# First attention of a hybrid diffusion step: queries kept in SBUF, key stacks moved into the last mLSTM scan, the prompt block's eight heads in one score tile

## The chip, the cores and the metric

The kernel runs on one core of one Trainium2 chip. The metric is the device time of one execution in microseconds (us), the median over the runs. TensorE (PE) multiplies matrices, VectorE (DVE) and GpSimd (POOL) do elementwise work and reductions, ScalarE (ACT) does activations and copies, SyncE (SP) issues most DMAs. PEld is the loading of weights into TensorE.

## The reference

One layer of a diffusion transformer over 128 prompt tokens and 1024 latent tokens, with attention heads and mLSTM heads side by side. In the reference's words, shortened:

```
h = rmsnorm(x, norm1_w) * (1 + sc1) + sh1
aq, ak, av, mq, mk, mv, mo, mg = split(h @ w_in)
aq = rmsnorm(aq, q_norm_w);  ak = rmsnorm(ak, k_norm_w)      # 8 query heads, 2 key heads, 64 wide
latent tokens:  aq = rope(aq); keys = [rope(ak), cache_k]; vals = [av, cache_v]   # 1024 + 128 keys
prompt tokens:  keys, vals = ak, av                                               # 128 keys, no rope
attn_o = softmax(aq keys^T / 8) vals
hm     = rmsnorm(mlstm_forward(..) + mlstm_backward(..)) * sigmoid(mo)            # 4 heads, 128 wide
x = x + g1 * ([attn_o, hm] @ w_out)
x = x + g2 * swiglu(rmsnorm(x, norm2_w) * (1 + sc2) + sh2)
```

Everything is float32. Most products are made from two halves (a high part and the rest), so one product is three matmuls.

## The kernel before, in words

The 1152 tokens are nine blocks of 128: block 0 is the prompt, blocks 1 to 8 are latent. Three blocks make a chunk. The program is built by Python generators that are woven into one another (`weave(main, side, n, m)` takes m steps of the side for n of the main), and a scheduler then orders the instructions of each engine; `hot()` raises the priority of what is written inside it. Tiles come from pools, where a tile with the same tag waits until an earlier one is no longer read.

The stages are: modulation of the conditioning, normalised input, key/value/gate projection, four mLSTM heads (the projection of one woven with the scan of the one before), then the part that the change touches:

- `linear_tok(w_q, ...)` projects the queries, 24 matmuls of 128x512 for a block. QFIRST (blocks 0 and 1, 2, 3) is woven with the last scan, `head_mlstm(3)`. QREST (4, 5 and 6, 7 and 8) comes later, woven with `key_stacks` and the first attention. `evac_q` copies a block out of PSUM (ACT, L696, tile `qraw`), `norm_rope` normalises and rotates it (a square on ACT L636, a sum on DVE L638, scaling on POOL L640, two half products on DVE L651 for each block, a product on POOL L657, a sum on DVE L658), and SP's queue writes the result to DRAM (`q_d`).
- `key_stacks` transposes the keys on PE and splits them into two halves in `kst` (casts on ACT L957 and L958, differences on DVE by the helper `sub`, L135).
- `attention(0)` treats blocks 0, 1 and 2. For a block it reads `qr` back from `q_d` by a DMA on ACT's queue, transposes it (PE L114) and splits it into `qT` (ACT L994, DVE L135). A head makes scores `S` on PE (L1016), a maximum (DVE L1018), an exponential (ACT L1019), a scaled half `ph` (ACT L1022), the rest `pl` (DVE L1023), and two transposing DMAs, `phT` and `plT`. Once both heads of a pair are through, the values follow on PE (L1040, L1041) into `po`. There is one score tile `S` of three banks and one bank for `po`; four banks `mm` serve everything else. For the prompt block a head is 128x128, for a latent block 128x1152.
- `prefill` multiplies the mLSTM half of the output projection for all nine blocks (PE L1138 to L1140). It evacuates through three small buffers (tag `t2`): DVE multiplies by the gate (L1095) and POOL adds to `x` (L1096). A product, its DVE evacuation and its POOL addition follow one another in each engine's own order.
- `attn_out(0)` adds the attention half for blocks 0 to 2 (POOL L1190), `norm2` normalises each block for the FFN (ACT L1251, transposes, L1259 on ACT for one column block in four of a half and L1261 on DVE for the others), and `gate_up_pair` starts the FFN early. The rest of attention 0 is taken in steps of `prefill` and `attn_out`, 0.7 of them for each step of attention. Attention 1 is woven into `attn_out` (0.3 of its steps for each one) and into the FFN groups behind it.

## Time and profile before

| | |
|---|---|
| median of 3 runs | 1628.43 us (1624.75, 1628.43, 2519.12) |
| profiled execution | 1623.65 us, its span 1621.9 us |
| mean granted PE clock | 0.973 |
| PE, DVE, ACT, POOL busy | 93%, 59%, 45%, 37% |
| DMA moved | 232.71 MB, of it HBM written 11.69 MB |

The span is what the profile shows of one execution, from its first instruction to its last; the execution's own time is 1.75 us longer. In the timeline a row gives the start, the duration, the engine, line, operation, `out<-in`, and in brackets how long the engine stood idle before it and what ended the idle time. In a table by windows each engine has its busy time and number of instructions; PEclk is the granted clock of TensorE (1.00 is full).

### The profile page before, as it was taken

How to read it: one execution, taken by the hardware profiler on the slowest of the kernel's cores; microseconds unless marked ns; L12 is line 12 of the kernel's file. 1: busy time of each engine (PE TensorE's matmuls, PEld its weight loads, DVE VectorE, ACT ScalarE, POOL GpSimd, SP SyncE). 2: the span in 40 equal slices, each digit the busy share in tenths (PEclk: the TensorE clock that was granted, in tenths of full speed). 3: DMA queues.
4: the chain of work that ended last, by engine and by line, in shares of the span. 5: the costliest groups of instructions: out<-in, count | busy, mean ns of one | idle time of the engine just before them, and what ended most of it. 6: DMA issues, size and time to landing. Idle time of an engine off the chain costs nothing. (4 is left out here: it accounts for less than half of the span.)

```text
span 1621.9 us, 23339 instructions
## 1 busy us (share of the span) xinstructions
PE 1513.3 (93%) x8688; PEld 1256.2 (77%) x8688; DVE 955.2 (59%) x1887; ACT 730.7 (45%) x1251; POOL 602.4 (37%) x363
## 2 busy tenths in 40 slices
PE   5899999899679867999999999999999999999996
PEld 2755666576347656998989999898898989899995
DVE  3844355847876667577663546777664474332445
ACT  3744343444444455545643344565552453333332
POOL 0411021413343414443445354443344444544443
PEclk8899999999889979999999999999999999999998
DMA  9345363302245755777763556787684445535441
GB/s 353 121 143 134 99 143 63 97 6 44 87 163 120 194 119 113 172 184 177 183 174 115 148 153 215 189 179 177 153 185 126 130 141 177 150 124 149 143 129 67
DMA packets 386311, 232.71 MB, mean 143 GB/s; under 512 B 169910, under 2 KB 346502, under 8 KB 386198
## 3 DMA queue, kind: packets, MB, share of 16 engines
q1 hardware_dynamic: 384342, 228.04, 52.6%
q10 hardware_dynamic: 1856, 3.19, 0.6%
q8 instruction: 68, 1.11, 0.3%
q14 instruction: 45, 0.37, 0.1%
HBM read 181.16 MB, written 11.69 MB: 119 GB/s over the span
## 5 line engine op out<-in xcount | busy, mean ns | idle before, releaser
L135 POOL TENSOR_TENSOR wlo<-raw,whi 128x1024 fp32r<-128x1024 f32 x146 | 360.9, 2476 | 435.6 <-ACT whi L152 404.5
L152 ACT CAST whi<-raw 128x1024 fp32r<-128x1024 f32 x219 | 224.1, 1025 | 357.9 <-DMA raw<-in_w_gu_dram 126.8
L1288 PE MATMUL mm<-aTl,whi 128*128 128x384 f32 (+2 forms) x1088 | 363.6, 334 | 0.7 <-POOL aTl L135 0.7
L1289 PE MATMUL mm<-aTh,wlo 128*128 128x384 f32 (+2 forms) x1088 | 363.4, 334 | 0.0
L1287 PE MATMUL mm<-aTh,whi 128*128 128x384 f32 (+2 forms) x1088 | 362.2, 335 | 0.8 <-DVE tn L1315 0.8
L1288 PEld LDWEIGHTS mm<-aTl,whi 128*128 128x128 f32 x1088 | 204.9, 188 | 1.7 <-POOL aTl L135 0.9
L1287 PEld LDWEIGHTS mm<-aTh,whi 128*128 128x128 f32 x1088 | 204.5, 188 | 2.2 <-DVE tn L1315 1.4
L1289 PEld LDWEIGHTS mm<-aTh,wlo 128*128 128x128 f32 x1088 | 204.9, 188 | 0.2
L135 DVE TENSOR_TENSOR wlo<-raw,whi 128x1024 fp32r<-128x1024 f32 (+1 forms) x73 | 86.7, 1188 | 145.5 <-ACT whi L152 145.3
L1106 PE MATMUL mm<-whi,hl 128*128 128x512 f32 x372 | 147.0, 399 | 1.4 <-DVE tn L1315 1.3
L1107 PE MATMUL mm<-wlo,hl 128*128 128x512 f32 x372 | 147.6, 398 | 0.0
L1108 PE MATMUL mm<-whi,hl 128*128 128x512 f32 x372 | 144.7, 397 | 0.7 <-POOL hl L135 0.7
L1023 DVE SCALAR_TENSOR_TENSOR pl<-pr,st,ph 128x1152 f16<-128x1152 f32 (+1 forms) x72 | 111.9, 1556 | 52.7 <-ACT ph L1022 51.0
L1019 ACT ACTIVATE pr<-S,st 128x1152 f32<-128x1152 f32 (+1 forms) x72 | 81.2, 1128 | 114.8 <-DVE st L1018 108.5
L488 PE MATMUL wi<-ipair,hT 128*128 128x384 f16 (+2 forms) x392 | 127.5, 326 | 2.9 <-ACT ipair L216 2.8
L489 PE MATMUL wi<-ipair,hT 128*128 128x384 f16 (+2 forms) x392 | 127.4, 325 | 0.0
L490 PE MATMUL wi<-ipair,hT 128*128 128x384 f16 (+2 forms) x392 | 126.8, 324 | 0.0
L135 POOL TENSOR_TENSOR hl<-tn,hl 128x384 fp32r<-128x384 f32 x66 | 82.8, 1256 | 106.9 <-ACT hl L1319 106.0
L1096 DVE TENSOR_TENSOR x<-x,t 128x512 f32<-128x512 f32 x102 | 116.7, 1167 | 0.8
L1315 DVE SCALAR_TENSOR_TENSOR tn<-tn,mm 128x384 f32<-128x384 f32 (+2 forms) x68 | 36.7, 540 | 136.3 <-PE mm L1289 93.5
L1016 PE MATMUL S<-kst,qT 128*128 128x384 f32 (+1 forms) x400 | 87.2, 353 | 13.5 <-ACT pr L1019 13.4
L1018 DVE TENSOR_REDUCE st<-S 128x1 f32<-128x1152 f32 (+1 forms) x72 | 88.8, 1233 | 16.7 <-PE S L1016 16.5
(353 smaller groups left out, 2639.5 us busy)
## 6 DMA issues: line engine op xcount, KB each, us to landing
raw<-in_w_gu_dram SPq DMA_DIRECT2D x132, 512.0 KB
raw<-in_w_down_dram SPq DMA_DIRECT2D x60, 512.0 KB
a<-in_w_ada_dram SPq DMA_DIRECT2D x32, 512.0 KB
gl<-g_d SPq DMA_DIRECT2D x36, 256.0 KB
aw<-in_w_ada_dram SPq DMA_DIRECT2D x16, 512.0 KB
iraw<-in_w_in_dram SPq DMA_DIRECT2D x32, 256.0 KB
raw<-in_w_out_dram SPq DMA_DIRECT2D x15, 512.0 KB
x<-in_x_sample_dram SPq DMA_DIRECT2D x13, 512.0 KB
```

The source lines that it names most:

```text
L135: (dve if eng == "dve" else pool).tensor_tensor(out=out, in0=full, in1=hi, op=ALU.subtract)
L152: nc.scalar.copy(hi[:, :n], raw[:, :n])
L488: mm(ps[:, :n], ah, wh[:, k % 2, c0 : c0 + n], start=(k == 0), stop=False)
L489: mm(ps[:, :n], ah, wl[:, k % 2, c0 : c0 + n], start=False, stop=False)
L490: mm(ps[:, :n], al, wh[:, k % 2, c0 : c0 + n], start=False, stop=(k == KD - 1))
L1096: eng.tensor_tensor(out=x1[:, cs], in0=x1[:, cs], in1=t, op=ALU.add)
L1106: mm(ps, ah, wh[:, k % 2, :], start=(k == 0), stop=False)
L1107: mm(ps, ah, wl[:, k % 2, :], start=False, stop=False)
L1108: mm(ps, al, wh[:, k % 2, :], start=False, stop=(k == nk - 1))
L1287: mm(ps, wh[:, k, :], th[:, k, :], start=(k == 0), stop=False)
L1288: mm(ps, wh[:, k, :], tl[:, k, :], start=False, stop=False)
L1289: mm(ps, wl[:, k, :], th[:, k, :], start=False, stop=(k == KD - 1))
```

## The change

- QFIRST loses block 3, which joins block 4 in QREST.
- The queries no longer go through DRAM: `evac_q` keeps them in tiles in SBUF (`q_first` for blocks 0 to 2, `qk` for each pair of the others).
- For QREST the half products and the last sum of `norm_rope` are issued on POOL instead of DVE.
- `key_stacks` is woven into the last scan; it was woven into QREST. The pools `po` and `S` are opened as soon as the scan's own PSUM pool closes, and the four `mm` banks stay open.
- The prompt block's eight heads become one tile: 16 score matmuls, one maximum, one subtraction, one exponential, one sum, one scaling, one copy, one difference, two transposing DMAs.
- `qT` has two buffers; the transposes of blocks 0, 1 and 2 are issued straight behind the scan, those of a later block when the block ahead is at its fifth head.
- The rate of `prefill` and `attn_out` beside attention 0 goes from 0.7 to 1.0.
- `norm2` gives ACT three column blocks in four for chunk 0; it was one.

```
-QFIRST = [(0, 1), (2,), (3,)]
-QREST = [(4,), (5, 6), (7, 8)]
+QFIRST = [(0, 1), (2,)]
+QREST = [(3, 4), (5, 6), (7, 8)]
...
-    psum = {"mm": es_b.enter_context(tc.tile_pool(name="pB", bufs=4, space=PSUM, reuse_waits="tile"))}
+    psum = {"mm": ctx.enter_context(tc.tile_pool(name="pB", bufs=4, space=PSUM, reuse_waits="tile"))}
...
-    def norm_rope(qp, cc, ss, x, nb, nh, w, rb):
+    def norm_rope(qp, cc, ss, x, nb, nh, w, rb, eng=dve):
...
-                dve.tensor_tensor(
+                eng.tensor_tensor(
                     out=t4[:, :, :, 16 * f : 16 * f + 16],
...
-        dve.tensor_tensor(out=x[:, skip:], in0=x[:, skip:], in1=t2[:, skip:], op=ALU.add)
+        eng.tensor_tensor(out=x[:, skip:], in0=x[:, skip:], in1=t2[:, skip:], op=ALU.add)
...
             act(qr[:, b - grp[0]], ps.rearrange("p (h d) -> p h d", d=HD), AF.Copy, scale=vsc[:, 2:3])
+            q_of[b] = qr[:, b - grp[0]].rearrange("p h d -> p (h d)")
...
-                for i, bb in enumerate(grp):
-                    dma(q_d[bb], qr[:, i].rearrange("p h d -> p (h d)"))
...
-    weave(linear_tok(w_q, 0, 512, ev_q, QFIRST), scan, 24, 60)
-    emit(scan)
...
+    ev_q = evac_q(qp, cc, ss, qw, lambda grp: q_first[:, grp[0] : grp[-1] + 1], dve)
+    weave(linear_tok(w_q, 0, 512, ev_q, QFIRST), beside((scan, 3.0), (key_stacks(), 0.2)), 16, 16)
+    es_a.close()
+    for name, bufs in (("po", 1), ("S", 1)):
+        psum[name] = ctx.enter_context(tc.tile_pool(name="p" + name, bufs=bufs, space=PSUM, reuse_waits="tile"))
+    emit(scan)
...
+        def turned(b):
+            qT = ap.tile([P, NQ, P], F32R, name=nm("qT"), tag="qT", bufs=2)
+            ps = bank()
+            for j in range(4):
+                transpose(ps[:, j * P : (j + 1) * P], q_of[b][:, j * P : (j + 1) * P])
...
+        def prompt_heads(qT):
+            S = psum["S"].tile([P, 3, 512], F32, name=nm("S"), tag="S")
+            for h in range(NQ):
+                for t in range(2):
+                    mm(S[:, h // 4, h % 4 * P : (h % 4 + 1) * P], qT[:, h, :], kst[h // 4][:, t, NB * P : (NB + 1) * P],
+                       start=(t == 0), stop=(t == 1))
...
+            dve.tensor_reduce(out=st[:, 0], in_=Sv, axis=AX.X, op=ALU.max, negate=True)
+            dve.tensor_tensor(out=p3, in0=Sv, in1=bc(st[:, 0], 2, [P, NQ, P]), op=ALU.add)
+            act(pr, pr, AF.Exp)
+            dve.tensor_reduce(out=st[:, 1], in_=p3, axis=AX.X, op=ALU.add)
+            dve.reciprocal(st[:, 0], st[:, 1])
+            dve.tensor_scalar(out=st[:, 1], in0=st[:, 0], scalar1=2.0 ** 14, scalar2=None, op0=ALU.mult)
+            dve.tensor_tensor(out=p3, in0=p3, in1=bc(st[:, 1], 2, [P, NQ, P]), op=ALU.mult)
+            nc.scalar.copy(ph, pr)
+            sub(pl, pr, ph, "dve")
...
+            dma_t(hT8, ph)
+            dma_t(lT8, pl)
...
+                    if h == 4 and b + 1 in blocks and b + 1 not in qTs:
+                        qTs[b + 1] = turned(b + 1)
...
-    weave(linear_tok(w_q, 0, 512, ev_q, QREST, bank), chain(key_stacks(), att), 24, 11)
+    next(att)
+    next(att)
+    ev_q = evac_q(qp, cc, ss, qw, lambda grp: ap.tile([P, 2, NQ, HD], F32, name=nm("qk"), tag="qk", bufs=3), pool)
+    weave(linear_tok(w_q, 0, 512, ev_q, QREST, bank), att, 24, 9)
...
-                    if j == 0 and c == 0:
+                    if j < 3 and c == 0:
...
-        due += 0.7
+        due += 1.0
```

Three places show what the scheduler makes of it. Each kernel's rows bear its own line numbers: in the changed kernel the helpers and `linear_tok` lie one line higher (L113, L134, L487), the rotation is L639, L650, L656 and L657 (before L640, L651, L657, L658), the addition to `x` is L1142 (before L1096), and L1025 to L1035 are in `prompt_heads`.

PE at the end of the last scan, before. `mm_4763` is block 4's query product, `mm_4773` and `mm_4792` are key transposes, `mm_4662` the scan's last product, `mm_4865` the first transpose of block 0's queries, `mm_4998` the first product of block 7.

```order
L846 MATMUL mm_4662<-va_4204,sd_4638 128x129 x2
L488 LDWEIGHTS hT_287
L488 MATMUL mm_4763<-ipair_4220,hT_287 128x512
...
L114 MATMUL mm_4773<-ident,kall 128x128 x4
...
L114 MATMUL mm_4792<-ident,kall 128x128 x4
...
L490 MATMUL mm_4855<-ipair_4231,hT_288 128x512
L114 MATMUL mm_4865<-ident,qr_4862 128x128 x4
L488 LDWEIGHTS hT_288
L488 MATMUL mm_4998<-ipair_4220,hT_288 128x512
```

PE at the same place in the changed kernel. `mm_4624` is the last key transpose, `mm_4682` the scan's last product, `mm_4730`, `mm_4740` and `mm_4784` are the transposes of blocks 0, 1 and 2, `mm_4793` and `mm_4794` the products of blocks 3 and 4, `mm_4936` and `mm_4937` those of 5 and 6, `S_4749` the prompt's scores.

```order
L113 MATMUL mm_4624<-ident,kall 128x128 x2
...
L844 MATMUL mm_4682<-va_4195,sd_4616 128x129 x2
L113 MATMUL mm_4730<-ident,q_first 128x128 x4
L113 MATMUL mm_4740<-ident,q_first 128x128 x4
L113 MATMUL mm_4784<-ident,q_first 128x128 x4
...
L489 MATMUL mm_4793<-ipair_4222,hT_278 128x512
L1025 MATMUL S_4749<-kst_4226,qT_4729 128x128 x2
...
L489 MATMUL mm_4794<-ipair_4218,hT_278 128x512
...
L1025 MATMUL S_4749<-kst_4227,qT_4729 128x128 x8
...
L489 MATMUL mm_4936<-ipair_4211,hT_278 128x512
L487 MATMUL mm_4937<-ipair_4211,hT_279 128x512
```

The key transposes now lie ahead of the scan's last product. Block 3's 24 products, which lay inside the scan before, stand behind it. The query transposes stand straight behind the scan instead of behind block 6, and the 16 prompt scores stand among block 4's products.

DVE behind the scan in the changed kernel. `rt_4698` and `ry_4697` belong to the root of the last mLSTM head's norm, `vs` to the values, `qT_4729`, `qT_4739` and `qT_4783` to the transposed queries of blocks 0, 1 and 2, `st_4771` and `pr_4768` to the prompt's softmax, `nrs_4910` to the norm of blocks 3 and 4.

```order
L130 SCALAR_TENSOR_TENSOR ry_4697<-rt_4698,ry_4697 128x9
L970 CAST vs<-vall 128x10x64 x2
L134 TENSOR_TENSOR qT_4729<-mm_4730,qT_4729 64x4x128
L134 TENSOR_TENSOR qT_4739<-mm_4740,qT_4739 64x4x128
L134 TENSOR_TENSOR qT_4729<-mm_4730,qT_4729 64x4x128
L134 TENSOR_TENSOR qT_4739<-mm_4740,qT_4739 64x4x128
L1032 TENSOR_REDUCE st_4771<-S_4749 128x8
L134 TENSOR_TENSOR qT_4783<-mm_4784,qT_4783 64x4x128
L1033 TENSOR_TENSOR pr_4768<-S_4749,st_4771 128x1024
L637 TENSOR_REDUCE nrs_4910<-nr_963_4908 128x16
L134 TENSOR_TENSOR qT_4783<-mm_4784,qT_4783 64x4x128
```

Before, twelve differences of `kst` stood at this place on DVE, and the first `qT` followed behind block 4's norm, the values and the norm's sum of blocks 5 and 6. Now the second half of `qT_4783`, which frees the bank of `mm_4784`, stands behind the reduction of blocks 3 and 4.

POOL at the start of `prefill` in the changed kernel. `qk_5033` and `qk_5178` are the queries of blocks 5 and 6 and of 7 and 8, `nr` their half products, `x_1019` and `x_1020` the residual sums with `t` from the DVE evacuation.

```order
L1142 TENSOR_TENSOR x_1019_5217<-x_1019_5217,t_1050_5327 128x512
L639 TENSOR_TENSOR qk_5033<-qk_5033,ry_5041 128x1024
L650 TENSOR_TENSOR nr_993_5057<-qk_5033,ss_4205 128x16x16 x3
L134 TENSOR_TENSOR kst_4227<-oT_4831,kst_4226 128x512
L650 TENSOR_TENSOR nr_993_5057<-qk_5033,ss_4205 128x16x16
L1142 TENSOR_TENSOR x_1019_5217<-x_1019_5217,t_1057_5362 128x512
...
L656 TENSOR_TENSOR qk_5033<-qk_5033,cc_4204 128x1024
L1142 TENSOR_TENSOR x_1019_5217<-x_1019_5217,t_1072_5448 128x512
L657 TENSOR_TENSOR qk_5033<-qk_5033,nr_993_5057 128x1024
...
L639 TENSOR_TENSOR qk_5178<-qk_5178,ry_5186 128x1024
```

Before, only the products of L640 and L657 stood here between the additions; now the half products (L650) and the sums (L657) of the rotation stand between them too.

More of the change, by code (lines that the diff above doesn't have):

```diff
@@ L98, in hybrid_step @@
     drp = ctx.enter_context(tc.tile_pool(name="drp", bufs=1, space=DRAM, reuse_waits="tile"))
-    es_b = ExitStack()
-    psum = {"mm": es_b.enter_context(tc.tile_pool(name="pB", bufs=4, space=PSUM, reuse_waits="tile"))}
+    psum = {"mm": ctx.enter_context(tc.tile_pool(name="pB", bufs=4, space=PSUM, reuse_waits="tile"))}
     def bank():
         return psum["mm"].tile([P, 512], F32, name=nm("mm"), tag="mm")
-    q_d = [drp.tile([P, 512], F32, name=f"q_d{b}") for b in range(NB)]
+    q_of = {}
     hm_d = drp.tile([TOK, 512], F32, name="hm_d")
@@ L686, in k_work, with evac_q @@
         yield
[L688 removed]
+    def evac_q(qp, cc, ss, qw, new, eng):
         held = {}
@@ new lines, in values @@
+        def values(i, j, nk, kv, rhs):
+            if j == 0:
+                oT.append(new_oT())
+            with hot(hv):
+                po = psum["po"].tile([P, 512], F32, name=nm("po"), tag="po")
+                for n in range(nk):
+                    v = vs[:, NB if nk == 1 else n, kv].rearrange("p t d -> p (t d)")
+                    for t in range(2):
+                        mm(po[:, 0:256], v, rhs(t, n), start=(n == 0 and t == 0), stop=(n == nk - 1 and t == 1))
+                ol = ap2.tile([64, 256], F32, name=nm("ol"), tag="ol", bufs=1)
+                act(ol, po[64:128, 0:256], AF.Copy, scale=vsc[64:128, 1:2])
+                for g in range(2):
+                    dve.scalar_tensor_tensor(out=oT[i][64 * g : 64 * g + 64, j, :],
+                                             in0=po[0:64, g * P : (g + 1) * P], scalar=vsc[0:64, 1:2],
+                                             in1=ol[:, g * P : (g + 1) * P], op0=ALU.mult, op1=ALU.add)
+            if j == 3:
+                done.add(i)
@@ L996, in attention @@
+        blocks = list(range(c * CB, (c + 1) * CB))
+        qTs = {}
+        with hot(ha):
+            for b in blocks[0:2] if c == 0 else blocks[0:1]:
+                qTs[b] = turned(b)
+        yield
+        for i, b in enumerate(blocks):
+            with hot(ha):
+                if b == 0:
+                    prompt_heads(qTs[b])
+                    qTs[2] = turned(2)
             yield
+            if b == 0:
+                continue
+            qT = qTs[b]
             for h in range(NQ):
+                kv = h // 4
+                if h % 2 == 0:
+                    while len(late) > 1:
+                        late.pop(0)()
@@ L1013, in attention @@
                     S = psum["S"].tile([P, 3, 512], F32, name=nm("S"), tag="S")
-                    for n in range(parts):
+                    for n in range(3):
                         for t in range(2):
-                            mm(S[:, n, 0:w], qT[:, h, :], kst[kv][:, t, c0 + n * w : c0 + (n + 1) * w], start=(t == 0), stop=(t == 1))
-                    Sv = S[:, 0:parts, 0:w]
+                            mm(S[:, n, 0:CT], qT[:, h, :], kst[kv][:, t, n * CT : (n + 1) * CT], start=(t == 0), stop=(t == 1))
@@ L1027, in attention @@
+                    dma_t(phT[:, h % 2, :, :], ph.rearrange("p a b -> p (a b)"))
+                    dma_t(plT[:, h % 2, :, :], pl.rearrange("p a b -> p (a b)"))
+                    if h == 4 and b + 1 in blocks and b + 1 not in qTs:
+                        qTs[b + 1] = turned(b + 1)
                 yield
-                if late and h % 2 == 1:
-                    late.pop()()
-                    yield
                 if h % 2 == 1:
-                    def values(phT=phT, plT=plT, kv=kv, nk=nk, b=b, i=i, j=h // 2):
-                        if j == 0:
-                            oT.append(new_oT())
-                        with hot(hv):
-                            po = psum["po"].tile([P, 512], F32, name=nm("po"), tag="po")
-                            for n in range(nk):
-                                vi = 9 if b == 0 else n
-                                v = vs[:, vi, kv].rearrange("p t d -> p (t d)")
-                                mm(po[:, 0:256], v, phT[:, :, n, :], start=(n == 0), stop=False)
-                                mm(po[:, 0:256], v, plT[:, :, n, :], start=False, stop=(n == nk - 1))
-                            ol = ap2.tile([64, 256], F32, name=nm("ol"), tag="ol", bufs=1)
-                            act(ol, po[64:128, 0:256], AF.Copy, scale=vsc[64:128, 1:2])
-                            for g in range(2):
-                                dve.scalar_tensor_tensor(out=oT[i][64 * g : 64 * g + 64, j, :],
-                                                         in0=po[0:64, g * P : (g + 1) * P], scalar=vsc[0:64, 1:2],
-                                                         in1=ol[:, g * P : (g + 1) * P], op0=ALU.mult, op1=ALU.add)
-                        if j == 3:
-                            done.add(i)
-                    late.append(values)
@@ L1051, in attention @@
+                    for _ in range(2 if len(late) > 2 else 1):
+                        if late:
+                            late.pop(0)()
+                            yield
+                    late.append(lambda i=i, j=h // 2, kv=kv, two=(phT, plT): values(i, j, NB, kv, lambda t, n: two[t][:, :, n, :]))
         late.pop()()
```

83 lines of the change are left out of this document (37 added, 46 removed).

## The prediction

> **What bounds the kernel now.** I read the page first: its chain of waits accounts only for the time from 1182 us on, so it says nothing on the stage that changes. The busy times by windows do.
>
> ```profile
> span 1621.9 us, 23339 instructions
> PE 1513.3 (93%) x8688; PEld 1256.2 (77%) x8688; DVE 955.2 (59%) x1887; ACT 730.7 (45%) x1251; POOL 602.4 (37%) x363
> ```
> ```profile
> core 0: us, PE busy (x) PEld busy (x) DVE busy (x) ACT busy (x) POOL busy (x), PEclk, DMA share, GB/s
> 390.90:414.60 23.70, 20.34 (x141) 15.42 (x140) 19.85 (x58) 12.76 (x43) 7.76 (x6) 1.00 0.12 37
> 414.60:457.50 42.90, 31.36 (x141) 14.91 (x140) 34.67 (x86) 15.55 (x38) 18.84 (x12) 0.88 0.33 112
> 457.50:500.00 42.50, 30.14 (x127) 22.84 (x126) 31.52 (x72) 19.14 (x42) 15.96 (x9) 0.84 0.54 158
> 500.00:554.40 54.40, 50.75 (x262) 41.52 (x261) 36.49 (x57) 27.27 (x36) 21.45 (x14) 0.97 0.64 144
> 554.40:628.00 73.60, 51.92 (x260) 41.31 (x259) 50.87 (x97) 41.33 (x58) 23.76 (x14) 0.84 0.63 137
> 663.00:1015.00 352.00, 351.19 (x1940) 323.86 (x1940) 214.78 (x308) 165.18 (x222) 151.45 (x76) 1.00 0.63 169
> 1040.00:1600.00 560.00, 556.36 (x3030) 513.98 (x3028) 293.99 (x406) 234.52 (x309) 253.02 (x123) 1.00 0.55 149
> ```
>
> From 663 us on PE is busy for 351.19 of 352 and 556.36 of 560 us, so work that is ready earlier there finds PE taken, and a microsecond won or lost ahead of it moves the end by one. Ahead of it PE has room. I cut the stage where the program does: A, the last scan (390.9 to 414.6); B, the query projection (to 457.5, where `prefill` begins); C, `prefill` (to 554.4); D, `attn_out` (to 628). In B, C and D PE stands idle for 11.5, 16.0 and 21.7 us, and half its clock is withheld for parts of the rest (0.84 to 0.88).
>
> What it waits for is seen in PE's timeline.
>
> ```profile
> 421.35 0.38 PE L490 MATMUL mm<-ipair,hT 128*128 128x512 f16 x1
> 424.88 0.58 PE L488 MATMUL mm<-ipair,hT 128*128 128x512 f16 x1 [3.15 <-ACT qraw L696]
> 427.39 0.46 PE L488 MATMUL mm<-ipair,hT 128*128 128x512 f16 x1
> 427.68 0.38 PE L489 MATMUL mm<-ipair,hT 128*128 128x512 f16 x1
> 436.32 0.38 PE L490 MATMUL mm<-ipair,hT 128*128 128x512 f16 x1
> 444.69 1.09 PE L114 MATMUL mm<-ident,qr 128*128 128x128 f32 x4 [7.99 <-DMA qr<-q_d]
> 471.12 0.69 PE L1016 MATMUL S<-kst,qT 128*128 128x128 f32 x2 [3.13 <-ACT pr L1019]
> 577.09 1.77 PE L1016 MATMUL S<-kst,qT 128*128 128x384 f32 x6 [2.80 <-ACT pr L1019]
> ```
>
> B holds a wait of 3.15 us for a free bank and one of 7.99 us for the query's way through DRAM. C begins with the prompt's heads, each waiting for the exponential of the one ahead (3.13 us), and D goes by heads of block 2 in the same way (2.80 us).
>
> At full clock the projection's matmuls follow at 0.216 us (427.68 to 436.32, 40 steps), so a block of 24 takes 5.2 us. Behind a wait they take 0.43: six from 424.88 to 427.39, about 1.3 us lost. [...]
>
> **B, what goes.** Both waits, 11.1 us, and what they slowed behind them. The round trip is certainly gone: no instruction reads or writes `q_d`. SP's queue loses those writes, and with them a wait that held all loads behind it:
>
> ```profile
> SPq L701 <- DVE qraw L658: 22.0, 3, 14.4
> ```
>
> It also issues two transposing DMAs for the prompt, not sixteen. I count that at nothing: weights arrived in time before.
>
> **A and B, what comes.** Three things.
>
> First, the scan. The twelve differences of `kst` move into it on DVE, and block 3's norm and rotation leave it.
>
> ```profile
> L135 DVE TENSOR_TENSOR kst<-mm,kst 64x512 fp32r<-64x512 f32 x8 | 5.5, 688 | 0.2
> L135 DVE TENSOR_TENSOR kst<-mm,kst 64x256 fp32r<-64x256 f32 x4 | 1.7, 422 | 0.1
> L651 DVE TENSOR_TENSOR nr<-qraw,ss 128x256 f32<-128x256 f32 x16 | 8.7, 594 | 3.3 <-POOL qraw L640 3.3
> L658 DVE TENSOR_TENSOR qraw<-qraw,nr 128x1024 f32<-128x1024 f32 x2 | 2.7, 1368 | 0.0
> L638 DVE TENSOR_REDUCE nrs<-nr 128x16 f32<-128x1024 f32 x2 | 2.4, 1220 | 0.8 <-ACT nr L636 0.8
> L636 ACT ACTIVATE nr<-qraw 128x1024 f32<-128x1024 f32 x2 | 2.1, 1052 | 4.2 <-DVE qraw L658 4.2
> L696 ACT ACTIVATE qraw<-mm,vsc 128x512 f32<-128x512 f32 x5 | 3.3, 685 | 6.5 <-PE mm L490 4.4 <-issue 2.0
> L994 ACT CAST qT<-mm 64x512 fp32r<-64x512 f32 x8 | 4.7, 582 | 5.9 <-PE mm L114 3.1 <-DVE qT L135 1.6 <-PE S L1016 1.1
> L135 DVE TENSOR_TENSOR qT<-mm,qT 64x512 fp32r<-64x512 f32 x8 | 5.5, 687 | 0.4 <-ACT qT L994 0.2
> ```
>
> 5.5 + 1.7 = 7.2 us come (these rows, and all by line that follow, are from 390 to 663 us where nothing else is said); the casts of `kst` go to ACT, busy for 12.76 of 23.7 us, and the transposes to PE, which has 3.4 us idle. Two half products (1.2), half of a 1.368 us sum, half of a 1.220 us reduction and the small root steps go, about 3.4 us. DVE was busy for 19.85 of A's 23.7 us, so the scan goes at its pace: the 3.8 us net are taken whole, and the scan ends at about 418 instead of 414.2. (Bounds: 0 if PE's slack hides them, 7.2.)
>
> Second, the first `qT`. Its tile's first cast on ACT waits for POOL: in the order it stands behind POOL's last product of the scan's output (L869). That row before, and two that stand close to it:
>
> ```profile
> 422.11 0.99 POOL L869 TENSOR_TENSOR hm<-hm,so 128x384 f32<-128x384 f32 x1
> 433.72 2.11 POOL L872 TENSOR_TENSOR hm<-hm,ry 128x1152 f32<-128x1152 f32 x1 [10.61 <-DVE ry L127]
> 423.38 0.17 DVE L129 TENSOR_TENSOR rt<-ry 128x9 f32<-128x9 f32 x1
> 433.74 2.11 DVE L129 TENSOR_TENSOR rt<-ry 128x8 f32<-128x8 f32 x1
> ```
>
> It ended 8.9 us behind the scan's end (423.1 against 414.2), so at about 426.9 now. A cast (0.58), block 3's evacuation, which stands between the casts on ACT (0.69), the second cast (0.58) and a difference (0.69) follow: block 4's products, which need that bank, start near 429.7. PE has the three transposes (about 2 us) and block 3's 5.2 us until 425.1 and two scores, so it waits about 4 us. (Bounds: 0, if another wait paces the tile, and the 7.99 us of before.)
>
> Third, the bank of `mm_4784`. Block 4's 24 products (5.2 us), 14 scores (2.4, estimated from 0.69 for two at half clock) and the slowed start (1.3) end at 438.6. `mm_4937` then waits for an evacuation (0.69), a square (1.05), a reduction (1.22) and a difference (0.69), with 0.2 to 0.3 between engines 4.6 us, of which three products of block 5 cover 0.65: about 4 us again, until 442.6. (Bounds: 0, if the difference goes ahead of the reduction, and 8, the largest wait of B.) Then 45 products remain of 5 and 6 and 48 of 7 and 8 (20.1 us), three latent heads' scores and some values (5.7, by the 1.77 us for six scores), 1.3 of slowed start. `prefill` starts at 442.6 + 27.1 = 469.7: **12 us later** than before. For that, all prompt heads and three latent ones are behind it.
>
> **C.** Busy time here is 30.14 + 50.75 = 80.9 us; with the slowed part taken out about 76. Six prompt heads go and one latent head comes (ten instead of nine), which makes 77.7.
>
> ```profile
> L1018 DVE TENSOR_REDUCE st<-S 128x1 f32<-128x1152 f32 x9 | 12.2, 1354 | 2.1 <-PE S L1016 2.0
> L1018 DVE TENSOR_REDUCE st<-S 128x1 f32<-128x128 f32 x8 | 2.3, 286 | 2.5 <-PE S L1016 2.5
> L1023 DVE SCALAR_TENSOR_TENSOR pl<-pr,st,ph 128x128 f16<-128x128 f32 x8 | 5.9, 745 | 3.9 <-ACT ph L1022 2.3 <-DMA plT<-pl 1.6
> ```
>
> The eight small chains on DVE, 2.3 + 5.9 and their small steps, 10.6 us, become two reductions (1.22 each), a subtraction (1.38), a scaling and a difference (1.37 each): 6.9 us, once. The first of these rows is of stage C. What made the first half of C slow, one small chain behind another, goes with them. The second half, 500 to 554.4, has only latent heads and 3.65 us idle in 54.4, 7%. At that share C has 5.6 us idle and some 2 of slowed clock: **85.5 us instead of 96.9**. (Bounds: 78 with none, 96.9 unchanged.)
>
> What rides on that is POOL, with twelve half products and three sums that it has not done before. The nearest rows are POOL's own products and additions.
>
> ```profile
> L657 POOL TENSOR_TENSOR qraw<-qraw,cc 128x512 f32<-128x512 f32 x4 | 5.1, 1268 | 4.3 <-DVE nr L651 4.3
> L1096 POOL TENSOR_TENSOR x<-x,t 128x512 f32<-128x512 f32 x18 | 27.3, 1520 | 50.0 <-DVE t L1095 44.5 <-DVE st L1021 3.5 <-DVE st L1020 2.1
> ```
>
> By L657 a half product of 256 columns is 0.63 us and a sum of 1024 is 2.54: 5.1 us for a pair, 15.2 for three. By DVE's rows it would be 3.75 a pair (11.2), by L1096 6.1 (18.2). I take L657's, the same operation on the same tile. POOL had 59.5 idle of 96.9 us in C, so the time itself is covered; what an addition that stands behind a rotation costs is the slow rival below. DVE loses 12 x 0.594 + 3 sums (1.37), 11.2 us, of which 1.9 in the scan.
>
> POOL may also hold DVE: a root step of 0.17 us took 2.11 beside L872, from the same start to the same end. With DVE busy for 68 of C's 96.9 us, 70% of the new 15.2 us, some 11, would fall on it. In C it has 28.9 idle for that, so I count nothing, and put the 11 into rival 3. [...]
>
> **D.** Eleven latent heads ran here (the first row is of this stage); their count is the pace, 73.6 / 11 = 6.7 us for each.
>
> ```profile
> L1018 DVE TENSOR_REDUCE st<-S 128x1 f32<-128x1152 f32 x11 | 14.9, 1353 | 5.3 <-PE S L1016 5.2
> L1261 DVE TENSOR_SCALAR fl<-mm,scale,shift 128x128 f32<-128x128 f32 x18 | 6.1, 402 | 0.0
> L1259 ACT ACTIVATE fl<-mm,shift,scale 128x128 f32<-128x128 f32 x6 | 2.5, 456 | 0.0
> ```
>
> In the order, three heads of block 2 are left behind `prefill` instead of seven, and block 3's four follow: seven, or **47 us, 26.5 less**. PE's own work for the stage is about 32 us and does not bind. The norm's 12 columns move 4.8 us off DVE and 5.5 onto ACT, both with room here. (Bounds: 33, PE's work; 73.6.)
>
> **Sum.** +12 - 11.4 - 26.5 = -26 us on the profiled 1623.65 (the span is 1621.9 of it): 1597.7. The runs shown lie 1.1 and 4.8 us above that execution, so about **1600**. A change within 2%, 1595.9 to 1661.0, can't be told from none.
>
> **Rivals.** (1) The start has no new waits: the cast does not wait so long, the bank is free in time, and the scan ends as before. For it: A has 3.4 us of PE idle, and ACT and DVE idle in B. Against: the two chains above, counted by rows. B's extra shrinks from 12 to 0: -38, 1586 (1588 with the runs' offset). (2) The tail is not paced by heads but by the norm of each block: a sum, a square (ACT), root steps, transposes and their evacuations follow one another three times whatever heads stand beside them. For it: DVE is busy for 50.87 us in D, of which eleven maxima are 14.9. Then D loses half, 13 us: 1611, or 1613 with the offset. (3) Slower: POOL becomes the pace of C. An addition to `x` waits behind a rotation step that waits for DVE's roots, the three `t2` buffers fill, DVE's evacuation stops, and PE's four banks with it. A pair's chain is 1.9 (L640's long form, estimated at 1.5 times L657's 1.27) + 5.1 + 2.5 = 9.5 us; three, with the 11 us in which DVE is held, are 39 us: C takes 124.5, the sum is +13, about 1639. It decides from C = 111.5, that is 26 us of stalls. Against it stands that additions and rotation steps alternate one by one, and POOL's idle 59.5 us. (4) That q still waits for DRAM is excluded by the order.
>
> **How the numbers follow.** Forecast 0.46 (own range 1592 to 1610), no new waits 0.23 (1580 to 1597), tail by the norm 0.24 (1606 to 1625), slower 0.07. The forecast has a fifth below 1595.9, the first rival nearly all: faster by over 2%, 0.31; slower by over 2% only where (3) is worse than its price, 0.03. The range from 1582 to 1625 leaves out the slow case and the ends of the two others.
>
> **What would show it.** No wait for `q_d`; `prefill`'s first product near 469 us; two PE waits of about 4 us, one ended by `qT`, one by the `qT` difference of block 2; `attn_out`'s first product about 85 us behind `prefill`'s; PE saturated from about 637 instead of 663. Wrong would be: PE waits in C ended by POOL's `x` (3), or D above 55 us (2).

## The result, and the profile after

The changed kernel took 1613.65 us (median of 7 runs, 1610.07 to 1618.44) against 1627.96 of the kernel before in the same comparison: a ratio of 0.993 [0.9904, 0.9956] (in brackets, here and below, its 95% interval), some 11 us. Two of the kernel before's seven runs were far slower than the rest (2519.12 and 1920.04) and are not in the ratio. Forecast were 28 (1628.43 to 1600). In a second comparison it was 0.9934 [0.9908, 0.996]. The profiled execution took 1617.88 us.

```profile
span 1616.1 us, 23209 instructions
PE 1521.3 (94%) x8688; PEld 1260.8 (78%) x8688; DVE 940.1 (58%) x1821; ACT 730.2 (45%) x1240; POOL 615.8 (38%) x376
```

Its span is only 5.8 us shorter, because its first 390 us, which the change does not touch, are 5.1 us longer. A wait for a load of the modulation weights near 250 us shows how such a difference comes about: in the four executions below PE waited 2.01, 3.73, 3.03 and 1.44 us for it, and behind the two longer waits the matmuls ran slowly (the granted clock of the next 5 us is 1.00 in the first and the last, 0.66 in the second and 0.50 in the third). The timelines of PE in the kernel before (twice), the changed kernel, and `free_last`, an experiment below:

```profile
251.01 0.63 PE L318 MATMUL mm<-a,silp 128*32 128x256 f32 x6 [2.01 <-DMA a<-in_w_ada_dram]
```
```profile
254.52 0.63 PE L318 MATMUL mm<-a,silp 128*32 128x256 f32 x6 [3.73 <-DMA a<-in_w_ada_dram]
```
```profile
252.68 1.07 PE L317 MATMUL mm<-a,silp 128*32 128x256 f32 x6 [3.03 <-DMA a<-in_w_ada_dram]
```
```profile
248.24 0.63 PE L317 MATMUL mm<-a,silp 128*32 128x256 f32 x6 [1.44 <-DMA a<-in_w_ada_dram]
```

I therefore count every execution from a point of its own, the 2400th matmul (389.4 us in the kernel before, 394.5 in the changed one), up to which the order of PE is the same. The changed kernel has other line numbers: L1184 to L1186 are `prefill`'s and `attn_out`'s products (before L1138 to L1140), L1075 the latent scores, L1078 the exponential, L1281 the square, L1297 the scaling to `y`, L1333 to L1335 the gate and up products.

The changed kernel by stages: the scan, the query projection up to `prefill`'s first product, `prefill`, `attn_out` up to its last product, and three pieces behind it.

```profile
core 0: us, PE busy (x) PEld busy (x) DVE busy (x) ACT busy (x) POOL busy (x), PEclk, DMA share, GB/s
398.40:421.80 23.40, 17.15 (x108) 14.30 (x108) 21.89 (x56) 16.93 (x56) 7.59 (x7) 0.88 0.01 2
421.80:473.70 51.90, 42.75 (x200) 22.29 (x200) 35.36 (x64) 21.92 (x36) 20.22 (x13) 0.92 0.45 108
473.70:563.50 89.80, 80.92 (x405) 65.97 (x405) 63.94 (x110) 42.48 (x56) 53.81 (x34) 0.94 0.63 147
563.50:616.40 52.90, 38.80 (x179) 30.95 (x178) 32.81 (x65) 31.01 (x49) 23.87 (x14) 0.81 0.60 135
616.40:635.50 19.10, 16.21 (x130) 14.84 (x128) 11.18 (x26) 9.27 (x17) 8.27 (x5) 0.97 0.63 160
635.50:648.20 12.70, 12.65 (x50) 12.38 (x51) 5.86 (x8) 5.78 (x9) 2.55 (x2) 0.50 0.47 87
648.20:663.00 14.80, 14.80 (x121) 14.42 (x121) 8.74 (x15) 10.96 (x16) 7.00 (x4) 1.00 0.51 121
```

The row to see is the sixth: PE is busy for 12.65 of 12.70 us, at a granted clock of 0.50 throughout. No stretch like it stands in the kernel before, and no wait is shown in it. PE's timeline has what leads up to it:

```profile
433.93 0.69 PE L1025 MATMUL S<-kst,qT 128*128 128x128 f32 x2 [4.39 <-DVE qT L134]
...
472.28 0.28 PE L999 MATMUL po<-phT,vs 128*128 128x256 f16 x1 [3.45 <-DVE oT L1003]
...
607.56 1.97 PE L113 MATMUL mm<-ident,y 128*128 128x128 f32 x8 [7.34 <-ACT y L1297]
...
632.27 1.27 PE L113 MATMUL mm<-ident,y 128*128 128x128 f32 x8 [0.93 <-ACT y L1297]
635.55 2.29 PE L1075 MATMUL S<-kst,qT 128*128 128x384 f32 x6 [2.00 <-ACT pr L1078]
640.01 0.41 PE L1335 MATMUL mm<-aTh,wlo 128*128 128x128 f32 x1
```

The waits on `qraw` (3.15) and on `q_d` (7.99) are gone, and 4.39 for the first `qT` stands in their place. In the tail PE waits for `y`, the norm of a block: 7.34 us for block 1. What holds it is seen on ACT, in its own order:

```profile
603.29 1.06 ACT L1281 ACTIVATE jk<-x 128x1024 bf16<-128x1024 f32 x1 [2.65 <-POOL x L1142]
...
606.79 1.33 ACT L1297 ACTIVATE y<-x,ry 128x512 f32<-128x512 f32 x2 [2.35 <-DVE ry L130]
...
609.82 1.23 ACT L1078 ACTIVATE pr<-S,st 128x1152 f32<-128x1152 f32 x1
```

The exponential at 609.82 had its maximum since 601.3 (on DVE from 599.91, 1.36 us). It stands behind the square and `y`, which wait for POOL and DVE; until it has read `S`, no next head can begin. On PE the products of block 2, whose operands were there at 602.0, stand behind block 1's `y` transposes as well.

To compare what is left to do and not what came last, I take the work of PE behind the 2400th matmul, each matmul weighed with 0.2165 us for 512 columns and in proportion for others (measured from one matmul to the next at full clock: 0.216 for 512 columns in f16, 0.23 in f32, 0.173 for 384, 0.11 for 128; with these instead the changed kernel's two numbers move by less than 0.1), and ask when an execution has done as much as the kernel before had at 628 and at 663 us. These numbers are worked out from the timelines; the kernel before's second profile differs by 0.1 at both places, the changed kernel's two by 1.6 and 2.3.

| kernel | ratio to the kernel before | first / last product of `prefill`, us behind the 2400th matmul | last of `attn_out` | equal work at 628 / 663 |
|---|---|---|---|---|
| before | 1 | 70.4 / 165.1 | 241.3 | 0 / 0 |
| changed (both profiles) | 0.993, 0.9934 | 79.3 / 169.0, 76.4 / 166.3 | 221.8, 220.3 | -15.8 / -9.5, -17.4 / -11.8 |
| norm2_free | 0.9875 | 78.9 / 167.9 | 219.3 | -21.0 / -23.1 |
| free_last | 0.986 | 76.6 / 165.9 | 219.1 | -18.6 / -20.9 |
| behind_one | 0.9859 | 78.5 / 168.7 | 213.4 | -23.2 / -21.7 |
| norm2_behind | 0.9873 | 78.2 / 169.0 | 217.8 | -19.8 / -13.2 |
| norm2_one | 0.9911 | 78.7 / 168.0 | 220.4 | -17.2 / -15.6 |
| add_dve | 0.9924 | 78.2 / 166.5 | 217.9 | -19.7 / -13.2 |
| rate07 | 0.9955 | 77.6 / 167.7 | 223.7 | -18.1 / -11.6 |
| att1_early | 0.9938 | 78.5 / 169.5 | 236.2 | -9.9 / -14.9 |
| kst_late | 0.9884 | 75.5 / 169.2 | 217.9 | -19.8 / -13.3 |
| prompt_apart | 0.9929 | 73.1 / 168.2 | 224.2 | -13.6 / -15.1 |
| behind_apart | 0.9938 | 73.2 / 165.9 | 222.9 | -14.8 / -11.4 |
| q_dram | 0.996 | 89.3 / 181.4 | 227.0 | -10.7 / -6.1 |
| rope_dve | 0.9954 | 79.5 / 178.6 | 227.8 | -9.9 / -3.4 |
| before_behind | 0.9967 | 70.5 / 164.6 | 232.7 | -4.0 / -4.5 |

### The profile page after: what moved, and what is told of

The parts are those of the page before. It is cut to its first block, busy times and chain, and to the rows that moved or that the text cites. A ratio compares the mean times of both kernels' runs of the same rounds, so it can differ in the third digit from the quotient of the medians.

```text
span 1616.1 us, 23209 instructions
## 1 busy us (share of the span) xinstructions
PE 1521.3 (94%) x8688; PEld 1260.8 (78%) x8688; DVE 940.1 (58%) x1821; ACT 730.2 (45%) x1240; POOL 615.8 (38%) x376
## 5 line engine op out<-in xcount | busy, mean ns | idle before, releaser
L134 POOL TENSOR_TENSOR wlo<-raw,whi 128x1024 fp32r<-128x1024 f32 x146 | 357.8, 2454 | 450.3 <-ACT whi L151 416.4
L1335 PE MATMUL mm<-aTh,wlo 128*128 128x384 f32 (+2 forms) x1088 | 366.4, 337 | 0.0
L1333 PE MATMUL mm<-aTh,whi 128*128 128x384 f32 (+2 forms) x1088 | 365.1, 337 | 0.9 <-DVE tn L1361 0.9
L1333 PEld LDWEIGHTS mm<-aTh,whi 128*128 128x128 f32 x1088 | 206.9, 190 | 2.1 <-DVE tn L1361 1.5
L1335 PEld LDWEIGHTS mm<-aTh,wlo 128*128 128x128 f32 x1088 | 207.0, 190 | 0.1
L134 DVE TENSOR_TENSOR wlo<-raw,whi 128x1024 fp32r<-128x1024 f32 (+1 forms) x73 | 88.2, 1208 | 132.9 <-ACT whi L151 132.7
L1082 DVE SCALAR_TENSOR_TENSOR pl<-pr,st,ph 128x1152 f16<-128x1152 f32 x64 | 109.5, 1711 | 46.7 <-ACT ph L1081 46.6
L487 PE MATMUL wi<-ipair,hT 128*128 128x384 f16 (+2 forms) x384 | 124.9, 326 | 2.8 <-ACT ipair L215 2.8
L488 PE MATMUL wi<-ipair,hT 128*128 128x384 f16 (+2 forms) x384 | 124.9, 325 | 0.0
L489 PE MATMUL wi<-ipair,hT 128*128 128x384 f16 (+2 forms) x384 | 124.4, 325 | 0.3 <-POOL hT L134 0.3
L134 POOL TENSOR_TENSOR hl<-tn,hl 128x384 fp32r<-128x384 f32 x66 | 81.9, 1241 | 96.5 <-ACT hl L1365 90.4
L1142 DVE TENSOR_TENSOR x<-x,t 128x512 f32<-128x512 f32 x102 | 116.1, 1158 | 0.8
L1078 ACT ACTIVATE pr<-S,st 128x1152 f32<-128x1152 f32 x64 | 78.3, 1223 | 80.4 <-DVE st L1077 77.6
L1141 DVE TENSOR_TENSOR t<-mm,gl 128x512 f32<-128x512 f32 x106 | 70.8, 683 | 40.6 <-PE mm L1154 15.8
L1077 DVE TENSOR_REDUCE st<-S 128x1 f32<-128x1152 f32 x64 | 86.5, 1351 | 13.2 <-PE S L1075 12.8
```

The source lines that it names most:

```text
L134: (dve if eng == "dve" else pool).tensor_tensor(out=out, in0=full, in1=hi, op=ALU.subtract)
L487: mm(ps[:, :n], ah, wh[:, k % 2, c0 : c0 + n], start=(k == 0), stop=False)
L488: mm(ps[:, :n], ah, wl[:, k % 2, c0 : c0 + n], start=False, stop=False)
L489: mm(ps[:, :n], al, wh[:, k % 2, c0 : c0 + n], start=False, stop=(k == KD - 1))
L1142: eng.tensor_tensor(out=x1[:, cs], in0=x1[:, cs], in1=t, op=ALU.add)
L1333: mm(ps, wh[:, k, :], th[:, k, :], start=(k == 0), stop=False)
```

## The experiments

Each ratio is to the kernel before, run in the same comparison. Where an experiment names heads that are through, it counts the latent ones by their maxima on DVE; a profile is of one execution.

**after_again**, the changed kernel itself.

> The changed kernel once more, as the reference of this group. Both theories: 0.990 to 0.996 of the kernel before. The theory that the late profile (the first 390 us, which the change does not touch, took 7.5 us longer in it) was one execution's accident expects a span of 1606 to 1612 us and the first 390 us within 3 us of the kernel before; the rival, that the change itself makes them longer, expects 5 us or more again.

0.9934 [0.9908, 0.996]; 1612.8 us of span. Its 2400th matmul is at 392.3, 2.9 us later than in the kernel before, where the first profile had 5.1 (the 7.5 of the expectation is not borne out): no trait of the change. **before_again**, the kernel before once more, settles it:

> The kernel before once more, profiled, to see how much its first 390 us, which the change does not touch, differ from one execution to the next. If the seven changed and part-changed kernels that were 1.4 to 10.7 us later there than the first profile show nothing but that, it is 2 to 8 us later too.

It is 5.2 us late at the 2400th matmul and has done equal work within 0.5 us of the first profile from there on, up to 1000 us; it took 1627.45 us.

**norm2_free**: does the tail go by the norm chain?

```
-                    a["rs"] += stats(x1[i : i + 1])
+                    stats(x1[i : i + 1])
+                    a["rs"] += [vsc[:, 0:1]]
```

> The first chunk's norm2 scales by a value that is there already, not by the root of its block's sum of squares; the squares and roots are still computed. Theory one (the tail behind prefill goes by the norm chain: addition on POOL, square on ACT, root on DVE, scaling on ACT, transposes): PE's waits for y, 2.92, 7.34 and 0.93 us in the changed kernel, shrink to 5 us or less together, and the time falls by 4 to 8 us against the changed kernel. Theory two (the tail goes by the number of heads that are left, 6.7 us each): no change beyond 2 us.

0.9875 [0.9846, 0.9905], 9 to 10 us faster than the changed kernel by the ratios, more than expected; 23.1 us of equal work at 663. Heads as the pace are out. But at 628 the lead is only 4 to 5 us above that of the changed kernel, of 11 to 14 at 663; the larger part arises behind it.

**free_last**: which of the three waits?

```
-                    a["rs"] += stats(x1[i : i + 1])
+                    r = stats(x1[i : i + 1])
+                    a["rs"] += [vsc[:, 0:1]] if i == 2 else r
```

> Only block 2's norm2 scales by a value that is there already; the others wait as changed. In the changed kernel PE runs at half clock for 12.6 us behind that wait (0.41 us for matmuls that take 0.28 at full clock). Theory one (that stretch is the second loss, about 5 us, and the short waits of 0.93 and 2.00 us ahead of it bring it on): 4 to 8 us faster than the changed kernel. Theory two (only the long wait for block 1 counts): within 2 us.

0.986 [0.983, 0.9889], 11 to 12 us faster than the changed kernel by the ratios, with the long wait still there:

```profile
597.86 1.97 PE L113 MATMUL mm<-ident,y 128*128 128x128 f32 x8 [7.33 <-ACT y L1298]
```

The half clock is not. Here the same products by windows in this kernel:

```profile
623.50:636.00 12.50, 12.14 (x106) 11.74 (x105) 8.90 (x13) 8.52 (x13) 3.93 (x2) 1.00 0.86 149
```

106 matmuls pass in 12.50 us, where the changed kernel had 50 in 12.70. So the short waits of 0.93 and 2.00 us ahead of that stretch, with the 6 us that it costs, weigh more than the wait of 7.34. The gain is above the 4 to 8 us expected; the 2.9 us of waits themselves belong to it.

**norm2_one** and **add_dve**: shorter or other ways through the chain.

```
-                    if j < 3 and c == 0:
+                    if j == 0 and c == 0:
```

> The changed kernel with one column block in four of the first chunk's norm2 on ACT instead of three. Theory one (the norm chain is the tail's pace, and it is its length that counts: three evacuations of 0.46 us on ACT or three of 0.41 on DVE are equally long): within 2 us of the changed kernel. Theory two (ACT, where the heads' exponentials stand behind the norm, is the tail's pace): 2 to 5 us faster.

0.9911 [0.9884, 0.9938]: the intervals overlap with the changed kernel's. In its profile only 6 of the 96 gate and up products of 128 columns are slow, that is over 0.40 us long (31 and 25 in the changed kernel's two), and the lead at 663 is 15.6 us, of which 11.5 are left at 1000. Theory two is not excluded.

```
-                    add_gated(x1[i], ps, gx[n] if b == 0 else gs[n], n, pool if gx is not None else dve)
+                    add_gated(x1[i], ps, gx[n] if b == 0 else gs[n], n, dve)
```

> The first chunk's residual addition in attn_out on DVE instead of POOL, in the changed kernel. Theory one (the norm chain paces the tail): the addition takes about 0.7 us instead of 1.3 to 2.4 and the chain is 1 to 2 us shorter for each block: 1 to 4 us faster than the changed kernel. Theory two (the chain is not the pace): within 1 us or slower, since DVE has more to do.

0.9924 [0.99, 0.9947], no difference that can be told. Its additions took 0.89 us each on DVE, the wait for block 1 fell from 7.34 to 6.74, and the slow stretch (28 products) stayed.

**norm2_behind**: the ready products of the next block ahead of the norm's transposes on PE. The norm's priority goes down with it, for chunk 0.

```
-            if then is not None and i > 0:
-                yield from then(i - 1)
             yield True
...
             if then is not None:
+                if i > 0:
+                    yield from then(i - 1)
                 with hot(200):
                     a["rs"] += stats(x1[i : i + 1])
...
-            with hot(800):
+            with hot(800 if c else 150):
```

> In the changed kernel a block's norm2 transposes stand on PE ahead of the next block's output products, which are ready while PE waits for y. Here norm2 of a block is issued behind the next block's products. Theory one (the tail's pace is PE standing in front of the norm chain with ready work queued behind): the waits for y, 11 us together, lose at least half, and the time falls by 4 to 8 us against the changed kernel. Theory two (it is the chain's end that counts, since gate and up products need its result): within 2 us.

0.9873 [0.9842, 0.9903]: 9 to 10 us faster than the changed kernel by the ratios. The profile shows less, 2 to 4 us more lead at 628, and the slow stretch again (30 products, 13.2 at 663). But it is of the slowest of the four executions, 1617.02 us at a mean granted clock of 0.969; the others took 1602.0 to 1609.88 us at 0.974 or 0.975. It was 7.3 us late at the 2400th matmul; whether the others have the slow stretch, no trace shows. **behind_one** adds norm2_one's line (`if j == 0 and c == 0:`) to it.

> Norm2 behind the next block's products, and one column block in four on ACT. Theory one (PE's waits for the norm chain and the half clock behind the last of them are two separate losses; the second did not show with one column block on ACT): both gains add, 5 to 10 us faster than the changed kernel, 0.984 to 0.990 of the kernel before. Theory two (they are the same loss): as fast as norm2_behind alone, whose ratio was 0.9873 with an interval of 0.984 to 0.990, or slower.

0.9859 [0.9834, 0.9883], 1602.32 us: the fastest that leaves nothing out, 11 to 12 us ahead of the changed one by the ratios. By the interval that is theory two's case too (norm2_behind's overlaps). Its PE timeline and windows behind the last norm:

```profile
593.31 1.60 PE L113 MATMUL mm<-ident,y 128*128 128x128 f32 x8
...
616.55 1.27 PE L113 MATMUL mm<-ident,y 128*128 128x128 f32 x8 [0.81 <-ACT y L1297]
618.98 1.32 PE L1075 MATMUL S<-kst,qT 128*128 128x384 f32 x6 [1.16 <-ACT pr L1078]
```
```profile
616.50:621.30 4.80, 2.99 (x17) 2.27 (x17) 3.83 (x11) 4.74 (x9) 1.27 (x1) 1.00 0.00 0
621.30:634.00 12.70, 12.35 (x105) 12.12 (x106) 6.00 (x9) 7.42 (x10) 4.97 (x3) 1.00 0.68 134
```

No wait for block 1 any more, and waits of 0.81 and 1.16 us behind the last did not bring on the half clock.

**before_behind**: norm2_behind's edit in the kernel before. Was the chain the pace there?

> The kernel before with norm2 issued behind the next block's products, nothing else. Theory one (the norm chain became the tail's pace only when the change had taken the heads out of it): within 3 us of the kernel before, since there its waits for y were 1.74 us. Theory two (it was the pace before as well): 4 to 8 us faster than the kernel before.

0.9967 [0.9951, 0.9982], 5 us faster than the kernel before: theory two, at its lower end. By the ratios, whose intervals are wide, norm2's place cost the kernel before about half of what it costs the changed one.

**att1_early**: other heads into the wait.

```
-        if i >= 6:
-            due += 0.3
+        if i >= 0:
+            due += 0.5
```

> The heads of attention 1 begin with the first step of attn_out instead of behind its sixth, at 0.5 steps instead of 0.3. Theory one (PE stands idle behind prefill for want of other work while the norm chain runs): the heads fill the 7.34 us wait, and the time falls by 4 to 9 us against the changed kernel. Theory two (heads are the pace): more heads in the tail lengthen it, 0 to 10 us slower.

0.9938 [0.9914, 0.9961], nothing. `attn_out` ends 14 to 16 us later, with 22 heads through instead of 18: no wait for `y` is left, but PE now waits for the heads (4.38 us for `pr` at 587.61 us, 5.80 for `phT` at 616.26). No product of 128 columns is slow, but the lead of 14.9 us at 663 passes: 9.7 at 680, 6.8 at 1000. Theory one misses; theory two's 0 to 10 us slower is not excluded by the time, only by norm2_free.

**rate07**: the old rate beside attention 0.

```
-        due += 1.0
+        due += 0.7
```

> The changed kernel with 0.7 steps of prefill and attn_out for a step of attention 0, as before. Theory one (more heads are through ahead of the tail at 0.7, but the norm chain paces the tail): within 3 us of the changed kernel. Theory two (the tail goes by the heads left, and 0.7 leaves fewer): 3 to 7 us faster.

0.9955 [0.9936, 0.9973], 3 to 4 us slower by the ratios, with overlapping intervals; theory two is out: 20 heads were through at the last product of `attn_out`, against 18, and it did not help. Its slow stretch is the longest (62 products), by windows:

```profile
641.50:658.00 16.50, 16.50 (x77) 16.25 (x77) 7.44 (x12) 8.38 (x12) 4.74 (x2) 0.50 0.49 105
```

**prompt_apart** and **behind_apart**: the prompt's heads one by one, as before, in the changed kernel and in norm2_behind.

```
         def prompt_heads(qT):
...
+            for h in range(NQ):
...
+                S = psum["S"].tile([P, 3, 512], F32, name=nm("S"), tag="S")
+                for t in range(2):
+                    mm(S[:, 0, 0:P], qT[:, h, :], kst[kv][:, t, NB * P : (NB + 1) * P], start=(t == 0), stop=(t == 1))
...
+                act(prv, Sv, AF.Exp, bias=st[:, 0:1], accum_out=st[:, 1:2])
```

> The prompt block's eight heads one after the other with a score tile each, everything else as changed. Theory one (the heads in one tile carry the gain of the start, since eight small chains stood one behind another): 5 to 9 us slower than the changed kernel. Theory two (the gain comes from the query's way through DRAM that is gone, and the small chains hide behind the projections of blocks 5 to 8): within 2 us of the changed kernel.

0.9929 [0.9902, 0.9957], as the changed kernel: theory two. By the trace it begins `prefill` 3 to 6 us earlier, takes 95.1 us for it instead of 89.8, and has 11 heads through at its end instead of 13. It is behind at 628 (13.6 against 15.8 and 17.4) and ahead at 663, since behind its last norm no half clock came: none of its gate and up products of 128 columns takes over 0.40 us.

> Norm2 behind the next block's products, and the prompt's heads one after the other. Theory one (the prompt's single tile did not count because the tail took its gain back; with the tail free it counts): 3 to 7 us slower than norm2_behind. Theory two (the small heads hide behind the projections of blocks 5 to 8 in any case): within 2 us of it.

0.9938 [0.9915, 0.9961], outside norm2_behind's interval: with that tail the single tile counts, by 2 to 19 us of the runs' intervals and 1.8 us of equal work at 663. I take the sign as shown, not the size.

**q_dram**: `evac_q` writes `q_d` again, `turned` reads it (and `qk` has two buffers instead of three, for the room that `qr` takes).

```
+            qr = ap.tile([P, 512], F32, name=nm("qr"), tag="qr", bufs=1)
+            nc.scalar.dma_start(qr, q_d[b])
...
```

> The changed kernel with the queries through DRAM again (written by SP's queue, read back by ACT's ahead of each block's transposes), all else as changed. Theory one (that round trip was the gain: its wait of 7.99 us and what it slowed): 6 to 11 us slower than the changed kernel, close to the kernel before. Theory two (the tail behind prefill, which goes by the norm chain, takes back what the start wins): at most 3 us slower.

0.996 [0.994, 0.9981], 4 to 5 us slower than the changed kernel by the ratios (the intervals just overlap), between the theories. PE's wait for `q_d` is there again, 9.34 us. At `prefill`'s first product it is 10 to 13 us behind, at its last 12 to 15, but with 16 heads through there instead of 13; measured by equal work (now with what the kernel before had done at 560 us) it is 6 to 9 us behind, and 3 to 6 at 663. Part of what the round trip costs is thus filled with heads, and the tail takes back some 3 us.

**kst_late**: the key stacks behind the scan.

```
-    weave(linear_tok(w_q, 0, 512, ev_q, QFIRST), beside((scan, 3.0), (key_stacks(), 0.2)), 16, 16)
+    weave(linear_tok(w_q, 0, 512, ev_q, QFIRST), beside((scan, 3.0)), 16, 16)
...
     emit(scan)
+    emit(key_stacks())
```

> The changed kernel with the key stacks behind the last scan instead of inside it. Theory one (their twelve differences on DVE, 7.2 us, stand ahead of the first query differences then, and what the scan saves is less): 3 to 7 us slower than the changed kernel. Theory two (the tail takes it back): within 2 us.

0.9884 [0.9837, 0.9932]: not slower. The scan's last product comes 8 us earlier without the stacks (18.4 us behind the 2400th matmul instead of 26.8 and 26.0), and PE then waits for them, 6.55 us in its timeline:

```profile
426.73 1.09 PE L113 MATMUL mm<-ident,q_first 128*128 128x128 f32 x4 [6.55 <-DVE kst L134]
```

Where they stand makes no difference that these runs can tell; the profile is of the slowest of the four executions (1619.21 us, the others 1604.11 to 1613.45) and has the slow stretch.

**rope_dve**: the rotation of blocks 3 to 8 back on DVE.

```
-    ... tag="qk", bufs=3), pool)
+    ... tag="qk", bufs=3), dve)
```

> The changed kernel with the half products and sums of the rotation on DVE again. Theory one (DVE was short of time in prefill, and 9.3 us less there count): 2 to 5 us slower than the changed kernel. Theory two (neither engine binds there; the order alone moves): within 2 us. If POOL was the pace of prefill, as the slow rival has it, it is 3 us faster or more.

0.9954 [0.9936, 0.9971], 3 to 4 us slower by the ratios, with overlapping intervals. The trace is clearer, and has theory one: `prefill` takes 99.0 us instead of 89.8 and ends 10 to 12 us later, with 15 heads through instead of 13. In equal work it is 6 to 9 us behind at 560 us and 6 to 8 at 663: the tail takes next to nothing back.

## Why the prediction was right or wrong

The sign was right, and the time lies in the range, but the gain is less than half of the forecast's. It is the price of the second rival, the tail by the norm (1613); its mechanism is part of the cause and not all of it, so that the time met the price is in part luck. By stages, forecast and measured (changed kernel's two profiles against the kernel before's first):

- *The scan 3.8 us later*: 1.6 and 0.8. Its last product came 26.8 and 26.0 us behind the 2400th matmul, 25.2 before. That DVE is its pace fits (the stacks cost 7.6 to 8.4 us for 7.2 of DVE, kst_late); but block 3's projection, which left it, was worth 6.8 (kst_late's 18.4 against 25.2) and not 3.4. That it had weighed on PE and DVE together is my reading, not shown.
- *A wait of 4 us for the first `qT`*: 4.39.
- *A wait of 4 us for a bank*: absent. I took `mm_4937` to need the bank of `mm_4784`; it ran without a wait at 444.5, 3 us ahead of the difference (447.76) that frees that bank. Instead a wait of 3.45 us for `po` stands right ahead of `prefill`. No run shows the 0.2 to 0.3 us between engines that stand in that term: in the kernel before's timelines ACT's cast at 445.81 starts 0.03 us behind the transposes that it waits for, and DVE's difference at 446.43 0.04 us behind the cast.
- *`prefill` 12 us later*: 5.6 and 3.5 by the transposes with which it begins (457.5 us before), 8.9 and 6.0 by its first product; the wait for `po` (3.45 and 2.73) lies between the two.
- *`prefill` in 85.5 us*: 89.8 in both from its first to its last product, from 94.6. It ends 3.9 and 1.2 us later than before with four more heads done, where 0.6 was forecast. That comes near, but for a reason that is half wrong: I gave it to the prompt's small chains and counted DVE's 9.3 us at nothing. With the small chains (prompt_apart) it takes 95.1 us, but begins earlier by 3 to 6; in equal work at 560 us that kernel is 1 to 4 us behind the changed one, and rope_dve 6 to 9. DVE's time was the larger term.
- *POOL 15.2 us more, bounds 11.2 to 18.2*: 11.5 + 9.2 = 20.7, above the upper bound, by the groups of the changed kernel from 440 to 570 us. It did not become the pace, and the slow rival did not come.

```profile
L650 POOL TENSOR_TENSOR nr<-qk,ss 128x256 f32<-128x256 f32 x12 | 11.5, 984 | 0.2
L657 POOL TENSOR_TENSOR qk<-qk,nr 128x1024 f32<-128x1024 f32 x3 | 9.2, 3079 | 0.1
```

- *The tail by the number of heads, 26.5 us*: the step that failed. From `prefill`'s last product to the work that the kernel before had done at 628 us it took 53.8 and 54.9 us instead of 73.6, where 47 was forecast: a gain of 19.8 and 18.7. `attn_out`'s last product came 19.5 and 21.0 us earlier, with 18 heads through where the kernel before had 20, so it wasn't the heads that held it. The rival of the norm chain names what did (norm2_free, norm2_behind). With the half clock behind its waits the chain costs 11 to 14 us of equal work at 663 (norm2_free's 23.1 against 9.5 and 11.8), close to the rival's 13; but the rival had all of it ahead of 628, and no half clock in it, and the sign named for it, this stage above 55 us, just did not come.
- *PE saturated from there, so that the lead stays*: PE was busy, but at half clock for 12.7 us. 50 matmuls passed where 105 or 106 pass at full clock in the two kernels above; the lead fell by some 6 us between 628 and 663, to 9.5 and 11.8. It was no term of the sum.

What is left of the difference between the forecast's 26 and free_last's and behind_one's 21 to 22 I have not traced.

That the half clock comes from the waits ahead of it fits all 18 traces. In each the granted clock changes only at points 3.41 us apart. I cut the time from 385 to 800 us at these points and take the pieces at full clock. Behind those in which PE was busy for less than 0.40 of the time the clock was halved in 93 of 93 cases, from 0.40 to 0.55 in 64 of 112, above in none of 1718; in the first profiles of the kernel before and of the changed kernel alone it is 13 of 13, 6 of 9 and none of 190. The piece ahead of the slow stretch has 0.45 and 0.41 in the changed kernel's two profiles; in the first of them it holds the whole wait of 0.93 us and half of that of 2.00. In free_last no stretch of that length has less than 0.89 there, wherever it is laid. In behind_one the two pieces with the waits have 0.61 and 0.62, and the worst position would have 0.42: that it kept the full clock was in part luck. Keeping PE busy there with useless products, which would test this directly, was not tried.

behind_one has the fixes that the experiments point to, 0.9859 of the kernel before.

## What to carry to other kernels

Ahead of a stage that the first engine saturates, ask of each microsecond won where it ends up: count equal work left, not the place of one product. An engine that stands in its order in front of a chain of four engines, with ready work queued behind, pays for the chain; here issuing the chain's consumer one block later won 9 to 10 us by the ratios. Add up short idle times that follow one another closely: here the clock was halved behind all 93 pieces of 3.41 us in which PE was busy for less than 0.40 of the time and behind none of 1718 with more than 0.55, and the half clock of 12.7 us stood behind waits of 0.93 and 2.00 us.
